# Latent attention operands stored in the layout of their tiles: 14 loads per head in place of 37, and two row transfers per item

## The chip, the cores and the metric

One Trainium2 chip, one core of it. The time is the device time of one launch in microseconds; the kernel before took 2618.85 us, the median of three runs (2615.45 to 2621.13). The profiled execution took 2617.4 us, of which 2615.3 us are the span that the trace covers.

## What is computed

One layer of a transformer trunk over 1024 latent tokens and 256 context tokens, float32: a half-step SwiGLU, two attention mixers on the same normalised input, a gated merge, and a second half-step SwiGLU. The change touches the second mixer, multi-head latent attention (MLA): eight heads, in each 64 channels of a query or key come from a low-rank projection ("nope") and 32 are rotated ("rope"). The rope part of the keys is the same for all heads.

```
def _mla_q(q_nope, q_rope):
    return jnp.concatenate([q_nope, q_rope], axis=-1)

def _mla_k(k_nope, k_rope):
    k_rope = jnp.broadcast_to(k_rope, k_nope.shape[:-1] + (k_rope.shape[-1],))
    return jnp.concatenate([k_nope, k_rope], axis=-1)

def _attend(q, k, v):
    s = jnp.einsum('bqhd,bkhd->bhqk', q * q.shape[-1] ** -0.5, k).astype(jnp.float32)
    p = jax.nn.softmax(s, axis=-1).astype(v.dtype)
    return jnp.einsum('bhqk,bkhd->bqhd', p, v)
```

## The kernel before

**Stages.** In order of time: adaLN vectors and the first SwiGLU (to about 1150 us), the input projections and the low-rank projections that make the queries, keys and values (to about 1350 us), neighbourhood attention (NA, to about 1472 us), MLA (1472 to about 1803 us), the merge, and the second SwiGLU. Queries, keys and values of both attentions go through DRAM: the projections store them, and the heads load them into tiles `w` of 128 x 1024 floats, of which there are 16. Every operand is split in a high part and a remainder (`hi`, `lo`), and products are made of high by high, high by low and low by high.

**A head's tiles.** An MLA head has seven `w` tiles: `qa`, `qb` for each half of the queries (`queries`, L1963), `k1`, `k2` (`leading_keys`, L1921) and `k3` (`first`, L1929). Rows 0 to 63 and 64 to 127 of a tile hold the same 64 operand rows, for the even and the odd blocks of 128 keys (`e` = 0, 1), so that two products run side by side in the two halves of the array. `qb` holds the rope rows and, in row 32 of each half, the negative of the row maximum: so the scores come out with the maximum already subtracted. Before, DRAM holds the projections' own layout (`qns`, `qrs`, `kns`, `krs`, L1528 to L1531), the constant rows stand in `edge`, and a head is put together by 37 transfers: 10 for each query half, 6 for the leading keys, 8 in `first` besides the queries, 3 for the values (`second`, L1939).

**An item** is one half of the queries of one head, so there are 16 items, 0 to 15, two for each head. Each runs in five parts p, 0 to 4 (`follow`, L2311, after the scores of each part). For an item i, part 0 does, in this order: the output of item i-4 (`out`, L2153: the product `o` times the broadcast inverse sums `rb`), the value product of item i-1 (`weigh`, 40 matmuls into a bank `bv`), the column sums of item i-2, a transpose of the columns (the negative maxima of item i+1 and the inverse sums of item i-3), the reciprocal (L2332), and `to_rows` (L2021): ScalarE copies the rows out of the bank (L2027) and issues DMAs from its own queue. Eight carry the maxima of item i+1 into row 32 of its `qb` (four pieces into each half, L2032), one carries the four rows of inverse sums to DRAM (L2035). `spread` (L2039) reads these back, broadcast over 64 partitions, as `rb` of item i-3.

**Maxima.** Before an item can start, its row maxima must be known. They come from products of the high parts alone (`maxima`, L2054, banks `bm`), eight steps an item, each reduced on VectorE (L2074). These steps run two items ahead: the steps of item i+2 are strewn over item i, the first after the second score product of part 0. So `qa`, `qb` of item i+2, and `k1`, `k2` of its head, must be there when item i begins.

**Order of the loads.** All loads and stores but `to_rows`' are issued in program order from SyncE's queue (SP): `first` and `second` of head h+1 in part 1 of item 2h, its successor's `queries(0)` in part 3, and `leading_keys` of head h+2 in part 0 of item 2h+1. With 16 tiles for two heads of seven, a load waits for its tile: `k3` of head h for the last scores of head h-2, `qa`, `qb` of its second half for that head's last value product, `k1`, `k2` of head h+1 for the first item of head h-1.

**Exponentials.** ScalarE turns each bank of scores into exponentials (L2111), ten of 128 x 512 an item, and PE cannot write scores into a bank before ScalarE has read it. `finish` (L2133) adds the last of them for the sums, on VectorE.

Of the kernel before, what the change touches and what calls it, by code (L numbers as in the profile page):

```python
# [15 lines left out]
P = 128  # L16
# [27 lines left out]
def hybrid_block(ctx: ExitStack, tc: tile.TileContext, a: dict, out: bass.AP):  # L44
# [1459 lines left out]
    def edge_rows():  # L1504

        x, y = T2(), T2()
        pool.memset(x[0:1, :], 1.0)
        pool.memset(y[0:32, :], 0.0)
        for h in range(2):
            c = slice(h * 512, h * 512 + 512)  # L1510
            store(edge[0:1, c], x[0:1, :])
            store(edge[1:33, c], y[0:32, :])
# [22 lines left out]
    def spill(pb, rows, n, dst, c0, scale=1.0):  # L1535
# [8 lines left out]
        store(dst[0, :, c0:c0 + n], f32(hi[:rows, :n]))  # L1544
        store(dst[1, :, c0:c0 + n], f32(lo[:rows, :n]))
# [77 lines left out]
    def q_heads(ci, cn):  # L1623
# [11 lines left out]
        for i in range(4):  # L1635
# [6 lines left out]
            for s, y in enumerate((hi, lo)):  # L1642
                store(qns[i][s, :, c0:c0 + 512], f32(y))
            if i in (1, 2):
                pb = PA()
                for j in range(4):
                    turn_(pb[:, j * P:(j + 1) * P], qr[:, j * 256 + (i - 1) * P:j * 256 + i * P], ident)
                spill(pb, P, 512, qrs[i - 1], c0, MS)
            yield

    def kv_heads(ci, cn):

        c0, n = CHUNKS[ci]
        for i in range(4):
# [3 lines left out]
            spill(pb, P, n, kns[i], c0)  # L1658
# [12 lines left out]
        spill(pb, 32, n, krs, c0)  # L1671
# [239 lines left out]
    class MlaHead:  # L1911
# [9 lines left out]
        def leading_keys(self):  # L1921
            self.k1, self.k2 = W(), W()
            self.keys(0, self.k1, 0, 0, 5)
            for e in range(2):
                for u in range(2):
                    r = 64 * e + 32 * u
                    ld(self.slots(f32(self.k2[r:r + 32, 0:640])), self.blocks(krs[0], e))

        def first(self):  # L1929
            self.k3 = W()  # L1930
            for e in range(2):
                r = 64 * e
                ld(self.slots(f32(self.k3[r:r + 32, 0:640])), self.blocks(krs[1], e))
                ld(f32(self.k3[r + 32:r + 64, 0:640]), edge[0:32, 0:640])
            self.keys(1, self.k1, 640, 0, 3)
            self.keys(1, self.k2, 640, 3, 5)
# [18 lines left out]
        @staticmethod  # L1955
        def slots(x):
            return x.rearrange("p (j c) -> p j c", c=P)

        @staticmethod
        def blocks(x, e, lo=0, hi=5):  # L1960
            return x.rearrange("p (j e c) -> e p j c", e=2, c=P)[e][:, lo:hi, :]

        def queries(self, x):  # L1963
            h, c0 = self.h, 512 * x
            b, i = (h % 2) * 64, (h % 4) * 32
            qa, qb = self.q[x] = W(), W()
            rope_rows = lambda s: qrs[h // 4][s, i:i + 32, c0:c0 + 512]
            for e in range(2):
                r = 64 * e
                ld(f32(qa[r:r + 64, :]).rearrange("p (s c) -> p s c", s=2),  # L1970
                   qns[h // 2][:, b:b + 64, c0:c0 + 512].rearrange("s p c -> p s c"))
                ld(f32(qb[r:r + 32, 0:512]), rope_rows(0))
                ld(f32(qb[r + 32:r + 64, 0:512]), rope_rows(1))
            for e in range(2):
                r = 64 * e
                ld(f32(qb[r:r + 32, 512:1024]), rope_rows(0))
                ld(f32(qb[r + 32:r + 64, 512:1024]), edge[1:33, 0:512])

        def keys(self, s, x, o, lo, hi):
            b = (self.h % 2) * 64  # L1980
            for e in range(2):
                ld(self.slots(f32(x[64 * e:64 * e + 64, o:o + (hi - lo) * P])),
                   self.blocks(kns[self.h // 2][s, b:b + 64, :], e, lo, hi))
# [37 lines left out]
    def to_rows(i, pb):  # L2021
# [4 lines left out]
        rows = T2()  # L2026
        nc.scalar.copy(rows[0:hi - lo, 0:P], pb[0:hi - lo, 384:512])  # L2027
        if lo == 0:
            after = mla[i + 1]
            for e in range(2):  # L2030
                for t in range(4):
                    nc.scalar.dma_start(f32(after.hd.q[after.i % 2][1][64 * e + 32:64 * e + 33, 512 + t * P:640 + t * P]), rows[t:t + 1, 0:P])  # L2032
        if hi == 8:
            d = inverse[i] = DR([4, P])
            nc.scalar.dma_start(d, rows[4 - lo:8 - lo, 0:P])  # L2035
# [11 lines left out]
    class MlaItem:  # L2047
# [105 lines left out]
        def out(self):  # L2153
            h, rb, o = self.hd.h, self.rb, self.o
            if self.i < FAST:
                nc.vector.tensor_tensor(o, o, rb, op=ALU.mult)
            else:
                nc.scalar.copy(rb, self.pv[:, 256:512])
                nc.vector.tensor_tensor(o, self.pv[:, 0:256], rb, op=ALU.mult)

# [150 lines left out]
    def follow(i, p):  # L2311
# [31 lines left out]
        if p == 1 and i > FAST:  # L2343
            prev.out()
        if i == FAST + 2 and p == 4:
            mla[i - 3].out()
# [7 lines left out]
        if p == (0 if i % 2 else 4):  # L2354
# [30 lines left out]
    mla[-1].finish()  # L2385
# [266 lines left out]
```

## Time and profile before

| | |
|---|---|
| median of 3 runs | 2618.85 us |
| profiled execution | 2617.4 us, span 2615.3 us |
| mean granted TensorE clock | 0.986 |
| MLA stage, 1472.0 to 1803.2 us | 331.2 us, PE busy 259.84, clock 0.90 |
| transfers issued by SP in the program | 1838 |
| transfers issued by ScalarE | 133 (120 row transfers, 13 stores of inverse sums) |

The profile's page lists busy time by engine, a chain of work followed back from the last instruction, and groups of instructions by line. `w` is a tile of a head, `t` a scratch tile, `d` a DRAM buffer, `bs`, `bm`, `bv` are banks of PSUM, `xp` the exponentials, `kr` a constant tile whose columns are reused for maxima. PE is the matmul, PEld the weight load, DVE VectorE, ACT ScalarE, POOL GpSimd; SPq and ACTq are the queues from which SyncE and ScalarE issue DMAs.

### The profile page before, as it was taken

The numbers are of one execution on the slowest core, as the hardware profiler recorded it, in microseconds if no ns is written. First come the engines' busy times: TensorE is split into PE (matmuls) and PEld (weight loads), VectorE is DVE, ScalarE is ACT, GpSimd is POOL, SyncE is SP. The second block draws the span as 40 slices with busy tenths as digits, with TensorE's granted clock in tenths as the row PEclk, the third lists the DMA queues.
The fourth block names the chain that finished last, engine by engine and source line by source line (L and its number), as shares of the span: only waits on it lengthen the run. The fifth ranks groups of instructions, "written<-read, shape, count | busy, mean of one in ns | idle before, by whom it ended". The sixth has DMA issues, their size and how long they took to land.

```text
span 2615.3 us, 39404 instructions
## 1 busy us (share of the span) xinstructions
PE 2519.9 (96%) x14168; PEld 2087.4 (80%) x14168; DVE 1831.5 (70%) x3216; ACT 1126.5 (43%) x2058; POOL 288.1 (11%) x365
## 2 busy tenths in 40 slices
PE   8999999999999999999999877779999999999998
PEld 6888888888998888888888665557888888888887
DVE  4788986797775577862567545446886888767777
ACT  6622223446644743342547433233167422333444
POOL 1000000001100000000014455442011000000003
PEclk9999999999999999999999989889999999999999
DMA  8556553943765665746789543323956454326824
GB/s 301 168 173 193 177 165 129 326 129 129 272 216 172 234 201 194 241 169 144 249 255 252 136 104 85 100 55 128 340 173 217 152 167 151 123 97 222 285 73 161
DMA packets 276078, 474.67 MB, mean 181 GB/s; under 512 B 66678, under 2 KB 101354, under 8 KB 275884
## 3 DMA queue, kind: packets, MB, share of 16 engines
q1 hardware_dynamic: 271940, 472.06, 55.8%
q8 instruction: 112, 1.84, 0.3%
q14 instruction: 82, 0.67, 0.1%
q10 hardware_dynamic: 3944, 0.10, 0.1%
HBM read 355.35 MB, written 116.62 MB: 180 GB/s over the span
## 4 chain that ended last, share of the span: by engine, by line
PE 89%; DVE 3%; ACT 2%; ACTq 2%; DMA 2%; issue 1%; SPq 0%; POOL 0%; POOLq 0%; DVEq 0%
PE bs L157 37%; PE bm L157 28%; PE bv L157 21%; ACTq L2032 2%; PE bm L160 1%; PE bs L160 1%; PE bv L160 1%; DMA w<-t 1%; ACT xp L2111 1%; DMA w<-d 1%; ACT t L123 1%; DVE kr L2074 1%; DVE xv L123 0%; DVE t L2129 0%; DVE t L123 0%
## 5 line engine op out<-in xcount | busy, mean ns | idle before, releaser
L123 ACT CAST xu<-t 128x512 fp32r<-128x512 f32 (+1 forms) x270 | 161.0, 601 | 493.8 <-DVE t L123 352.2
L157 PE MATMUL bm<-xu,xu 128*128 128x512 f32 (+2 forms) x1572 | 366.6, 387 | 0.0
L157 PE MATMUL bs<-xv,xu 128*128 128x512 f32 x1488 | 357.4, 389 | 0.3 <-DVE t L123 0.3
L157 PE MATMUL bv<-xv,xu 128*128 128x512 f32 x1342 | 335.5, 389 | 0.0
L157 PEld LDWEIGHTS bm<-xu,xu 128*128 128x128 f32 x1572 | 288.0, 188 | 56.8 <-issue 0.3
L157 PEld LDWEIGHTS bs<-xv,xu 128*128 128x128 f32 x1488 | 279.2, 188 | 58.9 <-issue 1.1
L157 PEld LDWEIGHTS bv<-xv,xu 128*128 128x128 f32 x1342 | 251.9, 188 | 52.2
L157 PE MATMUL bs<-xv,xv 128*128 128x512 f32 x1086 | 265.9, 390 | 0.0
L123 DVE TENSOR_TENSOR xu<-xu,xu 128x512 fp32r<-128x512 f32 (+1 forms) x296 | 202.1, 687 | 73.6 <-ACT xu L123 71.9
L123 POOL TENSOR_SCALAR st<-st 128x1 f32<-128x1 f32 (+1 forms) x66 | 34.7, 526 | 1882.6 <-ACT t L123 1864.4
L157 PEld LDWEIGHTS bs<-xv,xv 128*128 128x128 f32 x1086 | 203.1, 188 | 41.7
L157 PE MATMUL bs<-w,w 64*128 64x512 f32 (+3 forms) x918 | 182.7, 405 | 46.7 <-ACT xp L2111 46.2
L157 PE MATMUL bs<-xu,xu 128*128 128x512 f32 (+1 forms) x972 | 226.2, 382 | 0.0
L123 DVE TENSOR_TENSOR t<-t,t 128x512 f32<-128x512 f32 (+2 forms) x278 | 185.3, 674 | 45.8 <-ACT t L123 36.7
L157 PEld LDWEIGHTS bs<-xu,xu 128*128 128x128 f32 x972 | 177.5, 188 | 35.6 <-issue 1.4
L123 DVE TENSOR_TENSOR xu<-t,xu 128x512 fp32r<-128x512 f32 (+1 forms) x270 | 179.4, 665 | 10.7 <-ACT xu L123 10.6
L157 PE MATMUL bm<-xv,xv 128*128 128x512 f32 x690 | 182.9, 390 | 0.0
L123 ACT CAST xv<-t 128x512 fp32r<-128x512 f32 x170 | 105.8, 622 | 165.4 <-PE bv L157 69.2
L157 PEld LDWEIGHTS bs<-w,w 64*128 64x128 f32 x918 | 119.5, 204 | 70.8 <-ACT xp L2111 53.9
L2074 DVE TENSOR_REDUCE kr<-bm 128x1 f32<-128x320 f32 x241 | 107.2, 484 | 94.0 <-PE bm L157 91.3
L123 DVE TENSOR_TENSOR xv<-t,xv 128x512 fp32r<-128x512 f32 x170 | 117.3, 690 | 65.8 <-ACT xv L123 65.4
L123 ACT CAST xu<-xu 128x512 fp32r<-128x512 f32 x218 | 132.6, 617 | 69.7 <-DMA xu<-in_wo 56.9
(267 smaller groups left out, 4067.7 us busy)
## 6 DMA issues: line engine op xcount, KB each, us to landing
d<-t SPq DMA_DIRECT2D x350, 256.0 KB, 2.7
t<-d SPq DMA_DIRECT2D x274, 256.0 KB, 3.7
xu<-in_f1w SPq DMA_DIRECT2D x59, 512.0 KB, 3.8
xu<-in_f2w SPq DMA_DIRECT2D x58, 512.0 KB, 3.6
t<-in_wada SPq DMA_DIRECT2D x112, 256.0 KB, 5.3
xv<-in_f1w SPq DMA_DIRECT2D x44, 512.0 KB, 5.6
xu<-in_winT SPq DMA_DIRECT2D x38, 512.0 KB, 4.7
w<-d SPq DMA_DIRECT2D x64, 256.0 KB, 5.7
```

Of the source, the lines that this page charges most:

```text
L123: return lambda *x, **y: pin(f(*x, **y))
L157: return pin(nc.tensor.matmul(o, s, m, start=start, stop=stop, skip_group_check=open_group[0]))
L160: return pin(nc.tensor.transpose(o, x, i))
L2032: nc.scalar.dma_start(f32(after.hd.q[after.i % 2][1][64 * e + 32:64 * e + 33, 512 + t * P:640 + t * P]), rows[t:t + 1, 0:P])
L2074: nc.vector.tensor_reduce(d[:, t, 2 * x + e:2 * x + e + 1], pb[e][:, 0:320], axis=AX.X, op=ALU.max)
L2111: nc.scalar.activation(self.part(kb), self.pb[e], AF.Exp)
```

## The change

The DRAM buffers get the layout of the tiles. The projections write more transfers: a spill of keys goes out in four stores in place of two (even and odd blocks apart), of rope keys in six in place of two, of rope queries in three in place of two, and the constant rows of `edge` are written into `qrs` and `krs` by eight larger stores. A head then loads in 14 transfers: `qa` in one of 128 rows for each query half, whose source is the same 64 rows twice, `qb` in two of 64 rows, whose source is two groups of 32 rows, the three pieces of keys in one each, whose source is the even and the odd blocks of 64 rows, the rope keys in one each for `k2` and `k3`, and the values in three as before.

The rows of maxima go in two transfers an item in place of eight, each of four rows of 128 into 512 columns of one row. They stand in columns of `kr` in place of a scratch tile. The store of the inverse sums moves from ScalarE's queue to SP's. `spread` stands in part 4 of every item, where it stood in part 0 of the odd ones. `finish` stands in part 0 behind the new `scale` (the multiplication of `out` by itself), where it stood between the score products of part 0.

```
-    qns = [DR([2, P, NLAT]) for _ in range(4)]
-    qrs = [DR([2, P, NLAT]) for _ in range(2)]
-    kns = [DR([2, P, NLAT + NCTX]) for _ in range(4)]
-    krs = DR([2, 32, NLAT + NCTX])
-    edge = DR([33, NLAT])
+    qns = [DR([P, 2, 2, 512]) for _ in range(4)]
+    qrs = [DR([2, P, 2, 1024]) for _ in range(2)]
+    kns = [DR([2, P, 2, 640]) for _ in range(4)]
+    krs = [DR([2, 64, 640]) for _ in range(2)]
...
-            spill(pb, P, n, kns[i], c0)
+
+            def put_keys(s, x):
+                for e in range(2):
+                    store(kns[i][s, :, e, c0 // 2:(c0 + n) // 2].rearrange("p (j c) -> p j c", c=P), halves(x, n)[e])
...
         def leading_keys(self):
             self.k1, self.k2 = W(), W()
-            self.keys(0, self.k1, 0, 0, 5)
-            for e in range(2):
-                for u in range(2):
-                    r = 64 * e + 32 * u
-                    ld(self.slots(f32(self.k2[r:r + 32, 0:640])), self.blocks(krs[0], e))
+            self.keys(0, self.k1, 0, 0, 640)
+            ld(f32(self.k2[:, 0:640]), krs[0].rearrange("e p c -> (e p) c"))
...
-            for e in range(2):
-                r = 64 * e
-                ld(f32(qa[r:r + 64, :]).rearrange("p (s c) -> p s c", s=2),
-                   qns[h // 2][:, b:b + 64, c0:c0 + 512].rearrange("s p c -> p s c"))
-                ld(f32(qb[r:r + 32, 0:512]), rope_rows(0))
-                ld(f32(qb[r + 32:r + 64, 0:512]), rope_rows(1))
+            ld(f32(qa[:, :]), qns[h // 2][b:b + 64, x].rearrange("p s c -> p (s c)").unsqueeze(0).broadcast_to([2, 64, 1024]))
             for e in range(2):
-                r = 64 * e
-                ld(f32(qb[r:r + 32, 512:1024]), rope_rows(0))
-                ld(f32(qb[r + 32:r + 64, 512:1024]), edge[1:33, 0:512])
+                ld(f32(qb[64 * e:64 * e + 64, :]), qrs[h // 4][:, i:i + 32, x, :])
 
         def keys(self, s, x, o, lo, hi):
             b = (self.h % 2) * 64
-            for e in range(2):
-                ld(self.slots(f32(x[64 * e:64 * e + 64, o:o + (hi - lo) * P])),
-                   self.blocks(kns[self.h // 2][s, b:b + 64, :], e, lo, hi))
+            ld(f32(x[:, o:o + hi - lo]),
+               kns[self.h // 2][s, b:b + 64, :, lo:hi].rearrange("p e c -> e p c"))
...
-        rows = T2()
-        nc.scalar.copy(rows[0:hi - lo, 0:P], pb[0:hi - lo, 384:512])
+        o = 64 + P * (i % 2)
+        rows = kr.rearrange("p a b -> p (a b)")[0:8, o:o + P]
+        nc.scalar.copy(rows[0:hi - lo], pb[0:hi - lo, 384:512])
         if lo == 0:
             after = mla[i + 1]
             for e in range(2):
-                for t in range(4):
-                    nc.scalar.dma_start(f32(after.hd.q[after.i % 2][1][64 * e + 32:64 * e + 33, 512 + t * P:640 + t * P]), rows[t:t + 1, 0:P])
+                nc.scalar.dma_start(f32(after.hd.q[after.i % 2][1][64 * e + 32:64 * e + 33, 512:1024]), rows[0:4])
         if hi == 8:
             d = inverse[i] = DR([4, P])
-            nc.scalar.dma_start(d, rows[4 - lo:8 - lo, 0:P])
+            put(d, rows[4 - lo:8 - lo])
...
-            if 0 <= i - 4 < FAST - 1:
-                mla[i - 4].out()
+            done = mla[i - 4] if 0 <= i - 4 < FAST - 1 else None
+            if done:
+                done.scale()
+            if prev:
+                prev.finish()
+            if done:
+                done.out()
...
-        if p == (0 if i % 2 else 4):
+        if p == (0 if i == FAST + 2 else 4):
             spread(i)
...
                 item.scores(p, lo, hi)
-                if i and lo + p == 0:
-                    mla[i - 1].finish()
```

Three places show how this moves instructions. First, SP's queue in the loads of one head (head 5), from `k3` on. Before, `w_17106` is `k3`, `w_16866` and `w_16867` are `k1` and `k2`, `w_17115` and `w_17116` are `qa` and `qb` of the second half:

```order
L135 DMA w_17106<-d_386 32x5x128
L135 DMA w_17106<-d_387 32x640
L135 DMA w_17106<-d_386 32x5x128
L135 DMA w_17106<-d_387 32x640
L135 DMA w_16866<-d_384 64x3x128 x2
L135 DMA w_16867<-d_384 64x2x128 x2
L135 DMA w_17115<-d_378 64x2x512
L135 DMA w_17116<-d_381 32x512 x2
L135 DMA w_17115<-d_378 64x2x512
L135 DMA w_17116<-d_381 32x512 x3
L135 DMA w_17116<-d_387 32x512
L135 DMA w_17116<-d_381 32x512
```

Now, from the store of the inverse sums in an even item: `w_16961` is `k3`, `w_16732` and `w_16733` are `k1` and `k2`, `w_16965` and `w_16966` are `qa` and `qb`, `w_17031` and `w_17032` those of the next head's first half, `d_388` the values, and `t_16482` is the `rb` that this store feeds.

```order
L135 DMA d_16928<-kr 4x128
L135 DMA w_16961<-d_387 128x640
L135 DMA w_16732<-d_384 128x1x384
L135 DMA w_16733<-d_384 128x1x256
L135 DMA w_16965<-d_378 128x1x1024
L135 DMA w_16966<-d_381 64x1x1024 x2
L135 DMA w_16961<-d_388 128x6x64
L135 DMA w_16733<-d_388 128x2x64
L135 DMA y_13033<-d_388 128x2x64
L135 DMA w_17031<-d_379 128x1x1024
L135 DMA w_17032<-d_381 64x1x1024 x2
L135 DMA t_16482<-d_16928 64x256 x2
```

The transfers are fewer and larger, the store of inverse sums stands ahead of `k3`, and the read of `rb` behind the next head's queries; the next rows are the next item's store and then that head's leading keys.

Second, ScalarE at `to_rows` of one item, before (`bv` is the bank of the value product, `w_17189` a `qb`):

```order
L1770 COPY t_17031<-t_17031 64x256
L1773 CAST xo_13000<-t_17031 64x256 x2
L2027 COPY t_17749<-bv_17716 8x128
L2335 COPY t_17717<-bv_17716 128x256
L2032 DMA w_17189<-t_17749 1x16x8 x8
L2035 DMA d_17759<-t_17749 4x128
```

and now:

```order
L1794 CAST xo_13044<-t_16482 64x256
L1791 COPY t_16482<-t_16482 64x256
L1794 CAST xo_13044<-t_16482 64x256
L2027 COPY kr<-bv_17104 8x128
L2342 COPY t_17105<-bv_17104 128x256
L2031 DMA w_16621<-kr 1x4x128 x2
```

Nine issues have become two, in the same place.

Third, VectorE around the reciprocal of an odd item, before:

```order
L2129 TENSOR_TENSOR t_16786<-xp_16705 128x512
L2074 TENSOR_REDUCE kr<-bm_16788 128x1
L2074 TENSOR_REDUCE kr<-bm_16789 128x1
L2074 TENSOR_REDUCE kr<-bm_16805 128x1
L2074 TENSOR_REDUCE kr<-bm_16806 128x1
L2156 TENSOR_TENSOR t_16135<-t_16135 128x256
L2332 RECIPROCAL st_16851<-bv_16820 128x4
L1774 TENSOR_TENSOR xo_12999<-t_16135,xo_12998 64x256 x2
```

and now:

```order
L2128 TENSOR_TENSOR t_16686<-xp_16585 128x512
L2073 TENSOR_REDUCE kr<-bm_16659 128x1
L2073 TENSOR_REDUCE kr<-bm_16660 128x1
L2073 TENSOR_REDUCE kr<-bm_16676 128x1
L2073 TENSOR_REDUCE kr<-bm_16677 128x1
L2155 TENSOR_TENSOR t_16071<-t_16071 128x256
L1795 TENSOR_TENSOR xo_13043<-t_16071,xo_13042 64x256 x2
L2339 RECIPROCAL st_16724<-bv_16693 128x4
```

The addition (L2129, now L2128) has kept its place on VectorE; the two subtractions of `out` have moved ahead of the reciprocal, and both times the multiplication by `rb` (L2156, now L2155) stands ahead of it.

More of the change, by code (lines that the diff above doesn't have):

```diff
@@ L1543, in spill @@
                                            op0=ALU.mult, op1=ALU.subtract)
-        store(dst[0, :, c0:c0 + n], f32(hi[:rows, :n]))
-        store(dst[1, :, c0:c0 + n], f32(lo[:rows, :n]))
+        for s, x in enumerate((hi, lo)):
+            put(s, f32(x[:rows, :n]))
     def tiles_of(ci):
@@ L1642, in q_heads @@
             for s, y in enumerate((hi, lo)):
-                store(qns[i][s, :, c0:c0 + 512], f32(y))
+                store(qns[i][:, ci, s, :], f32(y))
             if i in (1, 2):
@@ L1647, in q_heads, with put_rope @@
                     turn_(pb[:, j * P:(j + 1) * P], qr[:, j * 256 + (i - 1) * P:j * 256 + i * P], ident)
-                spill(pb, P, 512, qrs[i - 1], c0, MS)
+                def put_rope(s, x):
+                    for c in (0, 512) if s == 0 else (0,):
+                        store(qrs[i - 1][s, :, ci, c:c + 512], x)
+                spill(pb, P, 512, put_rope, MS)
             yield
@@ L1670, in kv_heads, with put_rope @@
             turn_(pb[:32, i * P:(i + 1) * P], kr[:, t, :], ident)
-        spill(pb, 32, n, krs, c0)
+        def put_rope(s, x):
+            for e in range(2):
+                for u in range(2 - s):
+                    store(krs[s][e, 32 * u:32 * u + 32, c0 // 2:(c0 + n) // 2].rearrange("p (j c) -> p j c", c=P), halves(x, n)[e])
+        spill(pb, 32, n, put_rope)
     raw = {}
```

46 lines of the change are left out of this document (23 added, 23 removed).

## The prediction

> **What bounds the kernel now.** I read the page first, then the stage of the change by windows, then the waits in it, and last the order of time in one item.
>
> ```profile
> span 2615.3 us, 39404 instructions
> 1472.00:1803.20 331.20, 259.84 (x2184) 194.41 (x2182) 159.97 (x329) 110.17 (x236) 153.58 (x123) 0.90 0.33 81
> PE bs L157 <- ACT xp L2111: 46.2, 14, 3.9
> PE bm L157 <- DVE kr L2074: 23.4, 19, 2.8
> ```
>
> The second row is the MLA stage: length, then busy time of PE, PEld, DVE, ACT, POOL, then granted clock, DMA share, GB/s. PE is idle for 71.4 of 331.2 us, and the two wait rows (total us, times, longest) explain 69.6 of that. The larger one is PE waiting for exponentials, about once an item. One item shows why:
>
> ```profile
> 1620.29 5.01 ACTq L2032 DMA_DIRECT2D w<-t  x8
> 1625.34 0.48 ACTq L2035 DMA_DIRECT2D d<-t  x1
> 1625.87 1.57 ACT L2111 ACTIVATE xp<-bs 128x512 f32<-128x512 f32 x3 [5.35 <-DMA w<-t]
> 1626.52 1.28 PE L157 MATMUL bs<-w,w 64*128 64x512 f32 x2 [2.95 <-ACT xp L2111]
> L2032 ACTq DMA_DIRECT2D w<-t x120: 504/600/1627, 1474.1 to 1780.0; - x120
> L2035 ACTq DMA_DIRECT2D d<-t x13: 247/484/720, 1540.1 to 1793.3; - x13
> ```
>
> ScalarE spends 5.0 us on issuing eight row transfers and 0.5 on the store, meanwhile computes no exponential, and PE runs out of banks. Loads are not the limit: the DMA share of the stage is 0.33.
>
> ```profile
> 1510.53 4.88 PE bv L157 x55
> 1749.34 6.55 PE bv L157 x55
> 1803.19 4.90 PE bv L157 x55
> 1429.51 28.50 SPq L135 DMA_DIRECT2D w<-d  x36
> ```
>
> The first three are value products on the chain (in items 2, 13 and after 15): 14 items in 292.7 us, 20.9 an item, 41.8 a head. The fourth is where SP begins with MLA's loads.
>
> **Row transfers: a gain.** 120 issues at 600 ns are 72.0 us. Thirty remain, each of four rows; the nearest row is the four-row store at 484 ns, so 14.5 us. The 13 stores (6.3 us) go to SP. ScalarE is freed of 63.8 us, 4.25 per item over 15 items. That is more than the longest PE wait (3.9), so up to 46.2 us can go; at least nothing, if another wait takes their place.
>
> **How a load is spread over the DMA engines: the cost on which I decide.** The 133 transfers of ScalarE's queue can be counted packet by packet:
>
> ```profile
> q1 hardware_dynamic: 271940, 472.06, 55.8%
> q10 hardware_dynamic: 3944, 0.10, 0.1%
> ```
>
> q10 is that queue. A row transfer is written as 16 pieces, a store as four rows. If each engine that takes part moves its pieces and adds one packet for completion, the count is 120 x (16 + 16) + 13 x (4 + 4) = 3944, exactly the row. Stores on all 16 engines would give 4100, on one engine 3905. So a transfer is cut along its outermost dimension and no deeper: four rows, four engines, though each row had 128 floats to share out.
>
> Before, a head's loads have 32, 64 or 128 rows outermost on both sides. After, nine of the 14 do not: `qa` reads [2 copies][64 rows], the three key pieces read [2 blocks][64 rows], the four `qb` read [2 parts][32 rows]. The tile side has 128 or 64 rows, but the copy must be cut into the same pieces on both sides, and the source's outermost dimension has two entries. I take it that these nine run on two engines. No run here has sides that differ like that, so this is the inference on which the forecast stands.
>
> By the Trainium skill, "DMA: Bandwidth & Descriptors", section "Why a DMA increments its semaphore by 16 and not by 1", a transfer from this kind of queue uses the largest number of engines up to 16 that divides the outermost counts of both sides, and these are the lowest-numbered ones. By that rule the sum below holds, and without it the 16-engine rival does; the trace agrees as far as its four-row stores go (3944).
>
> **What two engines can carry.**
>
> ```profile
> 850.00:860.00 10.00, 10.00 (x52) 8.37 (x51) 4.86 (x8) 5.63 (x10) 0.00 (x0) 1.00 0.92 367
> ```
>
> This window is one of the fastest: 367 GB/s at a share of 0.92 of 16 engines is 25.0 GB/s for a busy engine. Over the whole span q1 moves 472.06 MB in 55.8% of 16 x 2615.3 us: 20.2. I take 25.0, since the new pieces are of 1 to 4 KB and the other 14 engines are nearly idle.
>
> A head's nine transfers are `qa` 2 x 512 KB, `qb` 4 x 256, keys 320 + 192 + 128: 2688 KB, 2.75 MB, 1.376 MB per engine, 55.1 us. The rope keys and values (five transfers, 960 KB) stay on 16 engines; their sixteenth is 61 KB, 2.5 us. **So two engines are busy for 57.5 us per head, where a head takes 41.8 now.** At 20.2 GB/s it is 71.
>
> By the Trainium skill, the same page, section "Specifications", an engine moves about 27 GiB/s, 29.0 GB/s; this would make the 57.5 an estimated 49.6 and the sum some 63 us smaller. The window has 25.0, and I stay with it.
>
> **The floor of the stage.** If the two engines are never idle, eight heads take 460 us from 1429.5. The last query load ends 0.8 us before that (values of head 7) and takes about 2 us to land: 1890.7. The first maxima in item 13 need it (they are item 15's), and about 1 us later comes item 13's value product: 1891.7, where it was at 1749.34. From there to the last value product it was 53.9 us; two row steps fall in it, some 3 us of PE wait each, so 48. The last value product is then at 1939.7 in place of 1803.2: 136.5 us later.
>
> **What leaves the engines idle.** Three things in the new order tie loads to computing. The store of an even item's inverse sums now stands on SP ahead of `k3`, and waits for ScalarE's copy in part 0, some 8 us into the item; the whole next batch of loads is queued behind it. The read of `rb` for item 2h-5 stands behind `queries(0)` of head h+1, on the same engines, so it comes only when those have landed; the multiplication (L2155) stands on VectorE ahead of the reciprocal, behind that come ScalarE's copy, the next store on SP, and behind that the leading keys, perhaps 4.5 us in all. And the second multiplication, in the middle of the odd item, waits for an `rb` that is queued behind the leading keys, so up to 9 us more pass before the next even item. That is 0 to 21.5 us a head. A wait overlaps with loads still in the queue, so I take the middle, 12, over five heads (3 to 7, as the store begins with item 3): 60 us.
>
> Before, that read was cheap:
>
> ```profile
> DVE t L2156 <- DMA t<-d: 2.9, 3, 1.9
> ```
>
> **The projections' stores.** They grow by 44 transfers (keys 24, rope keys 12, rope queries 4, constants 4).
>
> ```profile
> 1259.90 2.07 SPq L135 DMA_DIRECT2D d<-t  x4
> 1250.00:1300.00 50.00, 50.00 (x313) 44.93 (x313) 32.62 (x73) 31.00 (x63) 0.00 (x0) 1.00 0.78 270
> 1354.98 7.56 DMA w<-d
> ```
>
> At 2.07 / 4 = 0.52 us they are 23 us of SP's time over some 120 us in which PE does not idle (50.00 of 50.00), so most is hidden by PE's own work. Behind them in the queue are NA's first loads, which are on the chain of waits at 1355 us: a delay of those would show. Nothing to 4 us; I take 1. A gain is excluded, since nothing there becomes shorter.
>
> **The addition and the other moves.** The addition keeps its place on VectorE, and the maxima's rows in `kr` free a scratch tile that nothing waits for. Cost nothing; if VectorE were late there, its 0.67 us would come back as PE's wait for reductions, which is 23.4 us in all already. The SP issue that is saved (23 of 37 a head) is worth nothing as long as the engines behind the queue are the limit.
>
> **Sum.** 2617.4 (the profiled execution, 2.1 above its span and 1.5 below the median) + 136.5 + 60 + 1 = 2814.9, that is **2815 us**. The gain of the row transfers is in it only by the 6 us of the last items; elsewhere PE waits for loads anyway.
>
> **The rivals.** A measurement of this kernel can tell 0.2%, about 5 us, from no change.
>
> *Sixteen engines after all: faster.* If the hardware cuts these loads along the tile's 128 rows, or deeper, they are as fast as before and fewer, and the ScalarE gain comes through. For it speaks that every load of before ran so; against it that four rows of 128 floats were not cut deeper. PE's 46.2 us go. The stalls also cost clock:
>
> ```profile
> 1626.00:1627.00 1.00, 0.48 (x1) 0.28 (x1) 0.00 (x0) 1.00 (x3) 0.39 (x1) 0.70 0.02 2
> 1627.00:1628.00 1.00, 1.00 (x7) 0.99 (x8) 0.00 (x0) 0.94 (x2) 0.92 (x2) 0.50 0.00 0
> 1628.00:1629.00 1.00, 1.00 (x9) 0.81 (x8) 0.89 (x2) 0.00 (x0) 1.00 (x1) 0.50 0.49 89
> 1629.00:1630.00 1.00, 1.00 (x10) 0.91 (x8) 0.00 (x0) 0.34 (x1) 0.92 (x2) 0.59 0.13 42
> ```
>
> After the stall of the item above the granted clock (third number from the end) is 0.70, 0.50, 0.50 and 0.59 for a microsecond each, 1.7 us lost; 14 stalls make 24, of which I give a half, since VectorE's stalls remain. 46 + 12 less 5 for the reductions that then come late: 2617 - 53 = about 2565, between 2545 and 2600. This rival decides if the loads' time to land stays at a few us.
>
> *Two engines, never idle.* The floor alone: 2617.4 + 136.5 + 1 = 2755. For it: loads run far ahead where tiles are free, and SP is not blocked for long. Against it: the order above ties the next batch to part 0.
>
> *Two engines, and slower ones.* Packets read by two engines may not reach 25.0 GB/s. At 20.2, 13.3 us more a head: 2755 + 8 x 13.3 = 2861, and with a part of the idle time 2890.
>
> *It changes nothing:* sixteen engines, and the DVE waits (23.4 us now) or POOL's sums take the place of ScalarE's. ScalarE's freed 4.25 us would have to be lost fully; PE has 5 us of idle time an item, and VectorE is busy for 159.97 of 331.2 us only, so I see no work that long. 2613 to 2623.
>
> **How the numbers follow.** Two engines with the chain, 2815: 0.54. Two engines never idle, 2755: 0.22. Two slower engines, 2890: 0.09. Sixteen engines, 2565: 0.12. No change: 0.03. So faster 0.12, same 0.03, slower 0.85. The range should leave out 2 in 10: the faster case and no change make 0.15 of that. Its low end is the floor with a rate some 10% better (5.5 us less a head, 44 in all, 2711), taken as 2715; its high end the chain at its full 21.5 us a head (2755 + 108 = 2863) with some of the slower rate, 2890.
>
> **What would show it.** In the profile after: MLA's stage about 195 us longer, PE idle there for more than 200 us, waiting in `bm` and `bs` products for `w<-d` transfers; loads of 512 KB that land in 10 us and more, where 256 KB took a few; DMA share of the stage near 0.1 to 0.2 and not 1, since two of 16 engines are busy; fewer completion packets in q1. The row transfers at 30 issues near 0.5 us, and ScalarE's chain row for them all but gone. The idle time by the chain would show as VectorE's multiplication waiting for `t<-d` for tens of us in all, and SP waiting for ScalarE's copy into `kr`. The forecast is wrong at its root if 512 KB land in 3 to 5 us; then the faster rival holds. It is wrong in size if the stage's length divided by eight is near 57 (the floor) or over 80.

## The result, and the profile after

The changed kernel takes **2891.09 us** (median of 4 runs, 2889.45 to 2892.08), where the kernel before takes 2618.98 on the same chip: a ratio of 1.104, 95% interval 1.1021 to 1.1059. The forecast was 2815 in a range of 2715 to 2890: the right direction, 76 us too small, and just outside the range.

From the page after, the span, and of the DMA queues packets, MB and share of 16 engines:

```profile
span 2889.9 us, 39094 instructions
...
q1 hardware_dynamic: 260382, 474.37, 49.8%
...
q10 hardware_dynamic: 240, 0.06, 0.0%
```

By windows after: the MLA stage, ten microseconds in which it waits for loads, and a stretch of the projections (length, then busy time of PE, PEld, DVE, ACT, POOL, then granted clock, DMA share, GB/s):

```profile
1472.00:2077.50 605.50, 308.04 (x2391) 233.88 (x2391) 161.18 (x373) 123.99 (x262) 157.64 (x134) 0.71 0.15 50
1664.00:1669.00 5.00, 3.03 (x29) 2.50 (x26) 3.52 (x8) 2.51 (x5) 4.76 (x4) 1.00 0.13 48
1669.00:1674.00 5.00, 0.00 (x0) 0.00 (x0) 0.00 (x0) 0.00 (x0) 3.11 (x3) 0.60 0.13 50
1250.00:1300.00 50.00, 44.70 (x246) 37.70 (x245) 25.66 (x46) 27.84 (x57) 0.00 (x0) 0.93 0.88 262
```

The last value product starts at 2077.55 us, where it was at 1803.19: 274.4 us later, so the whole loss (2889.9 - 2615.3 = 274.6) lies ahead of it. PE is idle for 297 of the 605.5 us of the stage. While it stands still, the DMA share is 0.13: two of sixteen engines (0.13 x 16 = 2.1), at 24 to 25 GB/s each. The granted clock of the stage is lower too, 0.71 in place of 0.90.

The waits after (total us, times, longest):

```profile
PE bm L157 <- DMA w<-d: 136.9, 21, 15.1
PE bm L157 <- DVE kr L2073: 107.2, 18, 15.7
PE bm L157 <- issue: 44.3, 3, 15.6
PE bs L157 <- ACT xp L2110: 12.6, 1, 12.6
...
DVE t L2155 <- DMA t<-d: 154.4, 12, 27.8
...
ACT xu L123 <- DMA xu<-in_wuq: 12.6, 6, 3.5
```

PE's wait for exponentials has fallen from 46.2 to 12.6, as the change meant. Waits for loads have come in its place, and waits for reductions (L2073), which are themselves late: on VectorE ahead of them stands the multiplication by `rb` (L2155), which waited 2.9 us for its `rb` before and waits 154.4 now. (The last row belongs to the projections, experiment 4.)

One head on the timeline after, SP first (start, length, queue):

```profile
1660.37 0.27 SPq L135 DMA_DIRECT2D d<-kr  x1
1660.74 25.07 SPq L135 DMA_DIRECT2D w<-d  x8
1685.85 2.38 SPq L135 DMA_DIRECT2D y<-d  x1
1688.32 7.37 SPq L135 DMA_DIRECT2D w<-d  x3
1695.74 6.13 SPq L135 DMA_DIRECT2D t<-d  x2
1717.62 0.27 SPq L135 DMA_DIRECT2D d<-kr  x1
1717.99 1.11 SPq L135 DMA_DIRECT2D w<-d  x2
1719.19 1.23 SPq L135 DMA_DIRECT2D t<-d  x2
1742.10 0.27 SPq L135 DMA_DIRECT2D d<-kr  x1
```

And the other engines in the same head, with the idle time ahead of each and what ended it:

```profile
1681.62 0.63 PE L157 MATMUL bm<-w,w 64*128 64x320 f32 x2 [14.59 <-DMA w<-d]
1715.04 0.42 DVE L2155 TENSOR_TENSOR t<-t 128x256 f32<-128x256 f32 x1 [19.05 <-DMA t<-d]
1717.34 0.26 ACT L2027 COPY kr<-bv 8x128 f32<-8x128 f32 x1 [0.58 <-DVE st L2339]
1717.74 0.90 PE L157 MATMUL bm<-w,w 64*128 64x320 f32 x3 [14.80 <-DVE kr L2073]
1729.09 0.43 DVE L2155 TENSOR_TENSOR t<-t 128x256 f32<-128x256 f32 x1 [7.55 <-DMA t<-d]
1741.81 0.26 ACT L2027 COPY kr<-bv 8x128 f32<-8x128 f32 x1 [5.00 <-DVE st L2339]
```

Read it as a ring. The store goes out at 1660.4 and frees SP; the loads go out behind it, the queries of the next head and then the reads of `rb` last, at 1695.7. The read is done at 1715.0, and only then VectorE multiplies, ScalarE copies, SP stores (1717.6) and the leading keys follow. Their turn delays the second read until 1729.1. The next even item's store is at 1742.1, 81.7 us after the first. SP itself is held as well: it needs 25.07 us for the eight loads behind the store, so the reads are not even issued before 1695.7. Counted from the trace's packets, none of any queue is under way for 18.0 of these 81.7 us, 12.4 of them between the second read and the next even store.

### The profile page after: what moved, and what is told of

It is laid out like the page before. It is cut to its first block, busy times and chain, and to the rows that moved or that the text cites. A ratio compares the mean times of both kernels' runs of the same rounds, so it can differ in the third digit from the quotient of the medians.

```text
span 2889.9 us, 39094 instructions
## 1 busy us (share of the span) xinstructions
PE 2549.4 (88%) x14168; PEld 2111.0 (73%) x14168; DVE 1817.0 (63%) x3216; ACT 1128.9 (39%) x2058; POOL 286.8 (10%) x365
## 4 chain that ended last, share of the span: by engine, by line
PE 78%; DMA 13%; SPq 3%; DVE 2%; ACT 2%; issue 1%; POOL 0%; DVEq 0%; POOLq 0%; ACTq 0%
PE bs L157 33%; PE bm L157 24%; PE bv L157 19%; DMA w<-d 7%; DMA t<-d 4%; SPq L135 3%; PE bm L160 1%; ACT t L123 1%; PE bs L160 1%; PE bv L160 1%; DVE xv L123 1%; DVE xu L123 1%; ACT xu L123 1%; DMA d<-kr 0%; DVE kr L2073 0%
## 5 line engine op out<-in xcount | busy, mean ns | idle before, releaser
L157 PE MATMUL bm<-w,w 64*128 64x320 f32 (+1 forms) x572 | 118.5, 387 | 289.2 <-DMA w<-d 136.9
L157 PEld LDWEIGHTS bm<-w,w 64*128 64x128 f32 x572 | 85.2, 226 | 312.5 <-issue 126.3
L2073 DVE TENSOR_REDUCE kr<-bm 128x1 f32<-128x320 f32 x241 | 107.5, 485 | 212.3 <-PE bm L157 210.1
L157 PE MATMUL bs<-w,w 64*128 64x512 f32 (+3 forms) x918 | 187.5, 416 | 23.4 <-ACT xp L2110 12.6
```

The lines of the kernel that those rows point to most:

```text
L157: return pin(nc.tensor.matmul(o, s, m, start=start, stop=stop, skip_group_check=open_group[0]))
L2073: nc.vector.tensor_reduce(d[:, t, 2 * x + e:2 * x + e + 1], pb[e][:, 0:320], axis=AX.X, op=ALU.max)
```

## The experiments

Thirteen kernels, each compared with the kernel before on its chip. That kernel took 2616.68 to 2621.54 us (medians) on these chips, so a difference between kernels that ran on different chips is good to some 5 us. Two theories stood at the start: the two engines with three ties behind them (the forecast's), and the ties of the new order alone, whatever the engines. Rates of the two engines below 25 GB/s were the third possibility.

**1. All nine joined loads cut** (`qa` in two, `qb` and the key pieces in two each):

```
-            ld(f32(qa[:, :]), qns[h // 2][b:b + 64, x].rearrange("p s c -> p (s c)").unsqueeze(0).broadcast_to([2, 64, 1024]))
+            for e in range(2):
+                ld(f32(qa[64 * e:64 * e + 64, :]), qns[h // 2][b:b + 64, x].rearrange("p s c -> p (s c)"))
...
-                ld(f32(qb[64 * e:64 * e + 64, :]), qrs[h // 4][:, i:i + 32, x, :])
+                for s in range(2):
+                    ld(f32(qb[64 * e + 32 * s:64 * e + 32 * s + 32, :]), qrs[h // 4][s, i:i + 32, x, :])
...
-            ld(f32(x[:, o:o + hi - lo]),
-               kns[self.h // 2][s, b:b + 64, :, lo:hi].rearrange("p e c -> e p c"))
+            for e in range(2):
+                ld(f32(x[64 * e:64 * e + 64, o:o + hi - lo]), kns[self.h // 2][s, b:b + 64, e, lo:hi])
```

> The changed kernel with its nine joined loads a head cut so that both sides have 64 or 32 rows outermost: qa in two, each qb in two more, each piece of keys in two, 23 loads a head in place of 14; all else as in the changed kernel, the three ties too. Theory (the joined loads run on two engines, and their 57.5 us a head are the bound): the loads are back on sixteen engines, PE's 137 us of waits for w<-d and 107 us for reductions go, and the gain of the row transfers shows: 2565 us as in the first rival, plus some 8 us that the trace after shows in the projections, about 2573, within 2555 and 2610. Rival (the ties of the new order alone hold SP's queue, whatever the engines): the batches still start 81 us apart, and the time stays above 2800.

2592.33 us, ratio 0.990 (0.9875 to 0.9925). The same bytes from the same buffers, in more transfers, are 299 us faster: what cost the time is how a transfer is cut. Windows of this kernel:

```profile
1599.00:1604.00 5.00, 2.59 (x19) 1.70 (x16) 2.52 (x6) 1.55 (x3) 4.76 (x4) 1.00 1.00 222
1604.00:1609.00 5.00, 4.27 (x24) 3.13 (x26) 1.87 (x4) 1.08 (x2) 2.99 (x3) 0.66 1.17 232
```

All sixteen engines work (share 1.00 and above), 222 to 232 GB/s, where the joined loads had 48 to 50. The rival of the ties alone falls. It is 19 us over what was expected, though, which experiment 3 explains.

**2. The kernel before with the row transfers in two:**

```
-                for t in range(4):
-                    nc.scalar.dma_start(f32(after.hd.q[after.i % 2][1][64 * e + 32:64 * e + 33, 512 + t * P:640 + t * P]), rows[t:t + 1, 0:P])
+                nc.scalar.dma_start(f32(after.hd.q[after.i % 2][1][64 * e + 32:64 * e + 33, 512:1024]), rows[0:4, 0:P])
```

> The kernel before with one thing alone: the maxima of an item go in two row transfers of four rows in place of eight; loads, stores, layouts and order as before. Forecast: ScalarE's issues fall from 120 to 30, the 46.2 us of PE's wait for exponentials go and half of the 24 us of clock come back, less 5 for later reductions: about 2565 us. Rival (VectorE's reductions or POOL's sums take the place of that wait): 2600 to 2620.

2554.16 us, ratio 0.9752 (0.9731 to 0.9773): the fastest of the kernels that leave nothing out. Its MLA stage:

```profile
1470.00:1744.00 274.00, 242.13 (x2235) 188.39 (x2232) 158.63 (x331) 111.78 (x236) 153.99 (x123) 0.95 0.38 98
```

PE is idle for 31.9 of 274 us, where it was 71.4 of 331.2, and the clock has risen from 0.90 to 0.95. So the one part of the change that pays is the row transfers: 65 us by the ratio (57 of them in this stage), where the forecast's first rival had 53.

**3. The store of the inverse sums back on ScalarE's queue, with all loads cut:**

```
-            put(d, rows[4 - lo:8 - lo])
+            nc.scalar.dma_start(d, rows[4 - lo:8 - lo])
```

> The kernel that cuts all nine joined loads (2592), with the store of the inverse sums on ScalarE's queue again. It is 38 us over the kernel before with row transfers alone (2554): 9 us of that lie ahead of MLA, 30 in MLA. If the store on SP, which holds each head's first loads until 8 us into the even item, makes the 30: about 2563. If the cut loads of the new layout themselves are slower or the reads of rb in part 4 cost: 2580 to 2592.

2558.51 us, ratio 0.9774 (0.9753 to 0.9794), 34 us less than experiment 1. SP of experiment 1, then of this kernel, at about the same head:

```profile
1594.02 0.26 SPq L135 DMA_DIRECT2D d<-kr  x1
1594.33 7.58 SPq L135 DMA_DIRECT2D w<-d  x13
...
1633.77 0.26 SPq L135 DMA_DIRECT2D d<-kr  x1
1634.07 7.16 SPq L135 DMA_DIRECT2D w<-d  x13
```

```profile
1636.37 9.51 SPq L135 DMA_DIRECT2D w<-d  x13
1670.26 9.16 SPq L135 DMA_DIRECT2D w<-d  x13
```

In the first, thirteen loads stand behind the store; the batches come 39.7 us apart, in this kernel 33.9. So this tie costs time with sixteen engines as well, though each load is fast.

**4. The kernel of experiment 2, with 40 more stores in the projections** (keys cut in even and odd blocks, rope parts written twice; buffers as before):

```
-            spill(pb, P, n, kns[i], c0)
+            spill(pb, P, n, kns[i], c0, cut=2)
...
+            both = lambda z: z.rearrange("p (j e c) -> e p j c", e=2, c=P)
+            for e in range(2):
+                store(both(dst[s, :, c0:c0 + n])[e], both(x)[e])
+                if cut == 3 and s == 0:
+                    store(both(again[0][0, :rows, c0:c0 + n])[e], both(x)[e])
```

> The kernel before with the row transfers in two (2554), and with 40 more stores in the projections: each store of keys cut in its even and odd blocks, rope keys too and their high part twice, the high part of the rope queries twice; MLA's loads as before. The forecast took 1 us for these stores, at most 4: 2555 to 2558. The trace after shows the weight loads for the queries late behind them and PE idle for 5 of 50 us: then 8 to 9 us, 2562 to 2563.

2560.23 us (2556.37 to 2561.65), 6.1 over experiment 2 (4.7 by the ratios), whose own runs reach from 2552.43 to 2555.96: between the two guesses, nearer to the larger. PE's idle time in the projections is back, in this kernel 2.8 us of a stretch without any before:

```profile
1250.00:1300.00 50.00, 47.21 (x294) 42.04 (x294) 30.11 (x65) 29.54 (x62) 0.00 (x0) 1.00 0.80 237
```

The changed kernel has 5.3 there (44.70 of 50, above). What is late are the weights of the queries, which stand on SP behind the stores: ScalarE's wait for them is 2.1 us before, 7.6 here and 12.6 after (the row above). NA's first product starts at 1338.0 us in experiment 2, at 1341.8 here, at 1340.0 before and at 1348.1 after. So these stores make 2 to 4 of the 8 us by which the changed kernel is late there; where the rest comes from is not shown.

And 2560.2 against 2558.5 says that the new layout with loads cut (23 a head) and the old one (37) are equal, once both pay for the stores: the number of loads made no difference that shows.

**5. No ties:** the inverse sums are neither stored nor read, and the multiplication takes another operand.

```
-            put(d, rows[4 - lo:8 - lo])
+            del inverse[i]
...
-                nc.vector.tensor_tensor(o, o, rb, op=ALU.mult)
+                nc.vector.tensor_tensor(o, o, o, op=ALU.max)
```

> The changed kernel without the inverse sums of items 0 to 12: neither their store on SP nor the read of rb, and the multiplication by rb in these items is replaced by a maximum of the product with itself, same size and place (that part of the computation is left out). All loads as in the changed kernel, so the two engines stay and all three ties are gone. If the forecast missed only the idle time of the ties: the floor of 2755 plus 8 us of later start and 10 us of longer tail, about 2773. If it missed only the rate of the two engines (its 60 us of idle time were right): 2891 - 60 = about 2831. If the ties cost nothing: 2885 to 2891.

2777.11 us, ratio 1.0602 (1.0579 to 1.0625), on the first of the three expectations. So all ties together cost **114 us**, and the floor was right within 22. On the timeline of this kernel, the begin of MLA's loads and value products, one a head; then a window over six heads:

```profile
1439.48 55.01 SPq L135 DMA_DIRECT2D w<-d  x13
...
1652.01 4.73 PE L157 MATMUL bv<-xp,w 128*64 128x256 f32 x32
1710.46 4.52 PE L157 MATMUL bv<-xp,w 128*64 128x256 f32 x32
1769.02 4.26 PE L157 MATMUL bv<-xp,w 128*64 128x256 f32 x32
1828.24 5.35 PE L157 MATMUL bv<-xp,w 128*64 128x256 f32 x32
1886.92 5.03 PE L157 MATMUL bv<-xp,w 128*64 128x256 f32 x32
```

```profile
1532.10:1885.20 353.10, 199.97 (x1642) 153.31 (x1640) 112.19 (x260) 82.89 (x177) 128.26 (x101) 0.76 0.19 65
```

A head takes (1886.92 - 1652.01) / 4 = 58.7 us, where 57.5 were worked out for the two engines. Counted from the trace's packets, there is no moment in that window in which none is under way, and for 280 of 353 us exactly two are.

**6. and 7. The ties one at a time, loads joined.** First the store back on ScalarE's queue (the edit of experiment 3), then the reads too:

```
-                put(mla[i - 3].rb[64 * x:64 * x + 64, :],
+                nc.scalar.dma_start(mla[i - 3].rb[64 * x:64 * x + 64, :],
```

> The changed kernel with one thing undone: the store of the inverse sums goes out from ScalarE's queue again, as before; loads on two engines, reads of rb in part 4. SP then never waits for ScalarE's copy, so the loads' queue is no longer tied to part 0. Without any ties the time was 2777, with all three 2891. If the store on SP is the tie that carries the loss: 2775 to 2800. If the read of rb behind the next queries, and VectorE's multiplication that waits for it, carries it: 2850 or more. By the shares that the forecast gave them (8 us of 21.5): 2891 - 0.37 x 114 = 2849.

2837.97 us, ratio 1.0838 (1.0821 to 1.0854): 53 us of the 114 are gone; of the expected values, the one by the forecast's shares (2849) is the nearest. SP still waits for the store, now ahead of the reads; the waits of this kernel:

```profile
SPq L135 <- DMA d<-kr: 102.9, 12, 16.6
...
DVE t L2155 <- DMA t<-d: 105.5, 11, 18.7
```

> The changed kernel with the store of the inverse sums and the reads of rb both on ScalarE's queue (26 issues more there, at 0.5 us some 0.9 us an item); loads joined, on SP's queue. With the store alone there it is 2838, without store and reads 2777. If a read waits only behind what its own queue has issued: rb lands early, VectorE's 105 us of waits for it go, about 2780. If the two engines work off everything in order of issue whatever the queue: 2830 to 2850.

2811.44 us, ratio 1.0727 (1.071 to 1.0744): 27 less again, and neither expectation. VectorE's wait for `rb` is less than 105.5 us and far from none:

```profile
DVE t L2155 <- DMA t<-d: 68.6, 11, 11.1
```

The reads do overtake most of what lies ahead of them. By the semaphores in the trace, the slower of a head's two reads lands 17.0 us after its issue in experiment 6 (1683.55 to 1700.60) and 5.3 us after it here (1681.75 to 1687.04). What remains of the wait is the way from store to read: here as there this read is issued 4.2 us after its store. The other 34 us to 2777 (that wait, and 26 more issues on ScalarE) were not taken apart.

**8. One kind of load on two engines:** experiment 1, with `qa` joined as in the changed kernel.

> The same cut loads as in the kernel that cuts all nine, but qa stays joined: one transfer of 128 rows whose source is the same 64 rows twice, 512 KB on two engines by the theory, twice a head. Theory (what counts is the busy time of the two engines a head): 1.05 MB on two engines are 21 us at 25.0 GB/s, the other 2.6 MB on sixteen 6.6 us, 28 us in a head of some 38 us, so it fits, and the time is within 15 us of the kernel that cuts all nine. Rival (each transfer on two engines holds up what is queued behind it, however busy the engines are): 16 loads that land 10 us late, 100 us or more above it.

2669.21 us, ratio 1.0196 (1.0171 to 1.0221), 77 over experiment 1: the theory's 15 failed. Busy time that fits is not enough. PE waits for loads here, where the same row of experiment 1 has 15.8 us:

```profile
PE bm L157 <- DMA w<-d: 63.2, 22, 11.3
```

**9. The same with the store on ScalarE's queue:**

> The kernel in which qa alone stays joined (2669, 77 over the one that cuts all), with the store of the inverse sums on ScalarE's queue again. The two engines then have 28 us of work in a head of 36 to 40. If the loss came through the tie (a late qa delays the part that releases the next loads): the loads run ahead now, and the time is within 15 us of the kernel that cuts all nine with its store back. If each qa is late by itself, since its 512 KB take 10 us on two engines whenever they start: 60 us or more above it.

2636.58 us, ratio 1.0067 (1.0051 to 1.0082), 78 over experiment 3: it isn't the store. But VectorE waits for `rb` here:

```profile
DVE t L2156 <- DMA t<-d: 52.4, 11, 10.9
```

**10. and 11. Without the inverse sums:** the reference with all loads cut, and `qa` joined.

> The kernel that cuts all nine joined loads, without the inverse sums of items 0 to 12 (left out as in the kernel without ties): the reference for the kernels without inverse sums. With its store back on ScalarE's queue the cut kernel took 2558.5. VectorE's 10 us of waits for rb in it did not reach PE, so 2550 to 2558.

2548.18 us, ratio 0.9736 (0.9708 to 0.9764): 10 us under experiment 3, and 44 under experiment 1. So with all loads on sixteen engines the three ties cost 44 us together, where they cost 114 with nine loads on two: most of their cost needs the slow loads.

> The kernel in which qa alone is joined, without the inverse sums of items 0 to 12 (left out as in the kernel without ties). Two engines are busy for 28 us a head, under the some 34 us that a head takes when loads don't limit. With its ties qa alone cost 77 us, with the store back on ScalarE's queue still 78; VectorE's multiplication then waited 52 us for rb. If all of that comes through the read of rb behind qa on the same engines: within 15 us of 2558. If qa's 10 us to land are themselves too late for the maxima: 2600 or more.

2615.24 us, ratio 0.998 (0.997 to 0.9989), 67 over that reference: `qa` costs nearly as much without any read behind it. That is the time of the second expectation, but not its reason: PE waits for loads for 11.9 us in all, at most 1.0 at a time. Its longer waits are for reductions and exponentials, and ScalarE on the timeline shows what holds them:

```profile
PE bm L157 <- DVE kr L2074: 27.5, 18, 6.6
PE bs L157 <- ACT xp L2111: 20.2, 7, 7.1
...
1595.05 0.36 ACT L2343 COPY t<-bv 128x256 f32<-128x256 f32 x1
1600.12 1.27 ACTq L2032 DMA_DIRECT2D w<-kr  x2
1601.43 0.40 ACT L1794 CAST xo<-t 64x256 fp32r<-64x256 f32 x1 [6.03 <-DMA w<-d]
```

Its queue issues the row transfers at 1600.12, 4.7 us after the copy, and what it waited for is a load. The trace's records of the transfers name the semaphore that each one raises (start us, queue, semaphore, bytes of a piece):

```
1585.43 Sync   semaphore=106  4096  w<-d   (qa)
1586.06 Sync   semaphore=107  4096  w<-d   (qb)
1586.52 Sync   semaphore=108  4096  w<-d   (qb)
1586.99 Sync   semaphore=100  4096  w<-d   (qb)
1587.44 Sync   semaphore=102  4096  w<-d   (qb)
1587.96 Sync   semaphore=103  2560  w<-d   (keys)
1588.50 Sync   semaphore=104  2560  w<-d   (keys)
1589.22 Sync   semaphore=105  2560  w<-d   (rope keys)
1600.12 Scalar semaphore=106   512  w<-kr  (row transfer)
1600.81 Scalar semaphore=107   512  w<-kr  (row transfer)
```

The program has eight such semaphores and hands them round. A transfer waits until the one eight places ahead of it has landed, whatever its queue and tile: here the row transfer for `qa` of another head. The records show it directly: ScalarE's wait for semaphores 106 and 107 ends at 1600.08; 107 was complete at 1589.44, and 106 was raised twice, at 1600.03 and 1600.06, once by each of the two engines of `qa`. Six such waits of 4.7 to 6.7 us stand in this trace, once a head, and in each the exponentials stand still. In the traces of experiments 8 and 9 the row transfers wait so only once (5.8 us) and twice (7.4 us each), so there most of the 77 and 78 us has another cause; in 8 it is the wait for loads above, in 9 it stays open.

**12. `qb` ahead of `qa`,** nothing else, so that eight places ahead of the row transfers stand `qb` loads:

```
+            for e in range(2):
+                for s in range(2):
+                    ld(f32(qb[64 * e + 32 * s:64 * e + 32 * s + 32, :]), qrs[h // 4][s, i:i + 32, x, :])
             ld(f32(qa[:, :]), qns[h // 2][b:b + 64, x].rearrange("p s c -> p (s c)").unsqueeze(0).broadcast_to([2, 64, 1024]))
```

> The kernel in which qa alone is joined, without the inverse sums (2615), with one thing changed: the four qb loads of a query half are issued ahead of qa, where qa came first. In the trace of the 2615 run the row transfers on ScalarE wait once a head, 4.7 to 6.7 us, until a qa has landed that they don't touch: their semaphores are those of the transfers eight places earlier in the program, qa and the first qb. Theory (that wait is the loss): eight places ahead stand qb loads now, the waits go, and the time is within 15 us of the cut kernel without inverse sums, about 2558. Rival (qa is late for the maxima by itself): qa lands later still, 2615 or more.

2571.91 us, ratio 0.9826 (0.98 to 0.9852): 43 of the 67 us are gone (40 by the ratios), and with them all those waits. PE's waits for reductions and exponentials fall from 27.5 and 20.2 us to 8.4 and 1.6. `qa` is issued later than ahead of `qb`, and the kernel is faster; so the false wait is shown. Of the last 24 us over the reference, some belong to `qa` itself: PE waits 16.9 us for loads here, and 0.6 in the reference. The rest stays open.

**13. `qb` cut, `qa` and keys joined, without inverse sums:**

> The kernel without inverse sums (no ties, 2777), with the four qb loads a head cut in two each, so that they go on sixteen engines again; qa and keys stay joined (the inverse sums of items 0 to 12 are left out as there). Two engines carry 1.70 MB a head in place of 2.75: 34 us, and with a sixteenth of the other 2 MB 39 us, where all joined makes 57.5 and a head without any limit by loads takes some 34. Theory (busy time of the two engines sets the head's period): 2777 - 8 x 18 = about 2631. Rival (the loss is in each large load's own time to land, qa's above all): the two qa a head stay, so more than half of the 220 us over 2558 stays, 2670 or more.

2667.59 us, ratio 1.0175 (1.0156 to 1.0193), at the edge of the rival. But its value products are a steady head apart:

```profile
1623.24 3.67 PE L157 MATMUL bv<-xp,w 128*64 128x256 f32 x32
1667.31 3.67 PE L157 MATMUL bv<-xp,w 128*64 128x256 f32 x32
1711.97 3.67 PE L157 MATMUL bv<-xp,w 128*64 128x256 f32 x32
```

44.4 us, where 39 were worked out; by the packet records there are 1.9 us of 216 (1578 to 1794.4, where the loads end) in which none is under way. So busy time does set the period, and the sum of it was too small by 5 us: the 4 KB pieces took 0.206 us in the mean here and 0.166 in experiment 5, with the same median, 0.162. Why some take twice as long beside loads on all sixteen engines was not tried.

## Why the prediction was wrong, step by step

*Row transfers: right.* 30 issues are there, at 580 ns each and not 484. Alone they bring 65 us by the ratio of experiment 2, where 53 were forecast.

*Nine loads on two engines: right,* and shown by experiment 1 and the share of 0.13. The four-row transfers count out as before: 30 x (4 + 4) = 240 packets in q10. By the Trainium skill, "DMA: Bandwidth & Descriptors", section "Why a DMA increments its semaphore by 16 and not by 1", the count of engines must divide the outermost counts of both sides; the runs agree, from both directions. The sixteen-engine rival fell.

*25.0 GB/s and 57.5 us a head: right.* Experiment 5 has 58.7. The Trainium skill's 27 GiB/s of an engine (same page, section "Specifications") would make it an estimated 49.6, a rate that no window read here reaches (the best has 25.0). The rival of slower engines, 20.2 GB/s and 71 us (13.7 us more a head, where its sum has 13.3), fell with it, although its total of 2890 was nearest to the result: a right total is no proof of a mechanism.

*The floor of 2755: 22 us too low.* Without ties it is 2777. There the loads begin at 1439.5 in place of 1429.5 (10 us, of which the sum had 1; experiment 4's stores account for 2 to 4), eight heads at 1.2 us more make 10, and 3 are left over.

*The idle time: the step that failed.* "A wait overlaps with loads still in the queue, so I take the middle, 12, over five heads (3 to 7, as the store begins with item 3): 60 us" cost 114. The three ties were the right ones, each stands on the timeline where it was put. But they are in series, not beside the loads. Each batch starts only when the last link of the ring is done, and the reads of `rb`, the link that closes it, are by their place the last to land of all loads ahead of them. So when the multiplication can start, the engines have little left to overlap with. From 1654.68 to 1899.09 us, three heads by their value products, a head takes 81.5 us, 22.8 more than the 58.7 of the same loads without ties; five times 22.8 is the 114. For 18.1 us of each head no packet is under way, where experiment 5 has no such moment; the other 4.7 were not taken apart. The upper end of the term, 21.5 us a head, was nearer than the middle, and even it was passed by 1.3 us, for which no cause is shown. The false wait of experiment 11, which I had not seen, stands in the changed kernel's trace once, 8.1 us long. 60 to 114 makes 54 and the floor 22: the whole 76.

*The projections' stores: mis-sized,* 1 us taken, 4 at most; 6 measured for 40 of 44 (4.7 by the ratios), and a start of MLA's loads that is 8 to 10 us later, for which these 40 account in part only (experiment 4). I looked at NA's first loads behind the stores and not at the weights that stand between.

*The addition and the moves, fewer issues on SP: nothing,* as far as experiments 3 and 4 can tell (1.7 us between 23 and 37 loads a head).

## What to carry to other kernels

Count, for each transfer, what stands outermost on both sides before joining transfers: a source of [2][64] rows for a tile of 128 rows saves issues and loses fourteen of sixteen engines. Where a wait closes a ring (a store that waits for a result, a load behind it, a result that waits for the load), add its links up; only waits outside the ring overlap. Ahead of a late transfer ask too which later ones share its semaphore, as they wait for it without touching its data.

## What the runs showed that was not expected

- One slow transfer holds transfers of another queue: row transfers of 2 KB waited 4.7 to 6.7 us for a 512 KB load eight places ahead, and another order of five loads gave back 43 us.
- A load that occupies two engines for 28 of some 34 us a head still costs 67 to 78 us.
- The granted clock goes with the stops: 0.71 in the MLA stage after, 0.90 before, 0.95 with the row transfers alone. In that last kernel PE's idle time in the stage fell by 39.5 us and its busy time on the same work by 17.7, so the waits taken away were worth more than their length.
